# Weight copies and blocks of h formed in the projection of pair 0, in a gated pooling and attention block

## The chip, the cores and the metric

The kernel runs on 1 core of a Trainium2 chip. The metric is the device time of one execution in microseconds (us); of several executions the median is given. TensorE (PE in the profile) multiplies matrices, VectorE (DVE), ScalarE (ACT) and GpSimd (POOL) work on elements, SyncE (SP) only issues DMA transfers; ScalarE and GpSimd issue some as well. Each engine runs its own instructions in order and waits on semaphores for the others.

## What is computed

One decoder block over 1040 tokens (16 meta tokens and 1024 of the sequence) with 1024 features. All in float32:

```python
h = rmsnorm(x, norm_g)
proj = einsum('bld,dn->bln', h, w_in)
u_pool, z_pool, q, k, v, z_attn, f_logit, g_pool, g_attn = split(proj)
y_pool = causal_multiscale_pool(u_pool, pool_w, pool_scale) * silu(z_pool)
log_f = log_sigmoid(f_logit + b_forget)
y_attn = forgetting_attention(q, k, v, log_f) * silu(z_attn)   # 8 heads of 64, causal
merged = sigmoid(g_pool) * (y_pool @ w_up_pool) + sigmoid(g_attn) * (y_attn @ w_up_attn)
out = rmsnorm(x + merged @ w_out, final_norm_g)                # meta tokens dropped
```

In the attention, logit[t, s] = q_t.k_s / 8 plus the sum of log_f over s < j <= t. Before log_sigmoid, b_forget (the tile `bfb`) is added to the gate logits.

## The kernel before

Each float32 matrix product is made of three products of reduced float32 parts: hi x hi, hi x lo, lo x hi. So h is held in on-chip memory as `hh` and `hl` (the normalised tokens, high and low part, transposed), and each block of weights is loaded into `raw` and split by ScalarE (`whi`) and GpSimd (`wlo`).

The program has four stages.

1. **Front**, to about 62 us: the tokens are loaded (`xt`), normalised and transposed, and q, k and v of head pair 0 are projected in a list `todo` of twelve steps (q, k, v for four groups of tokens; `n` counts them). Then `gates()` projects the forget gates in three pieces (`pj<-hh,wfs`), copies them out (`fT`, VectorE), transposes them, adds `bfb` and forms the sums `negc`, which every logit needs. While that chain runs, TensorE is given fill work: q and k of pair 1 (`f_q`, `f_k`). The fill work writes two banks of PSUM in turn (`pj`, `PJ = 2`): q piece 1, q piece 2, then k pieces; a bank is free when ScalarE (`qa`) and VectorE (`ql`) have emptied it.
2. **16 attention units** (4 pairs x 2 heads x 2 halves of the queries), to about 430 us. The logits of a unit are made beside the softmax of the unit before, and TensorE's gaps are filled with projections: u and the gates g, whose pieces are evicted by ScalarE into staging tiles `st` (2 buffers) and stored to DRAM by SyncE (`sp_u`, `sp_gp`, `sp_ga`).
3. The remaining projections, by a Strassen-Winograd scheme of seven products (`g_prod`), to about 550 us. Its operands are sums of 512x512 blocks of h (`HS`) and of w_in (`GS`) in DRAM.
4. The up projections and the output projection, the latter by the same scheme with sums of blocks of w_out (`TD`).

The block sums for stages 3 and 4 are prepared during stage 2. `put` notes copies of weight blocks within DRAM; `move` hands them to ScalarE's queue after the exponentials (L612). `put_h` copies the high and low parts of a block of h to DRAM, where an adding transfer of GpSimd joins them; `put_neg` forms a negated block with ScalarE (L627) and GpSimd (L629). `add` is an adding transfer on GpSimd's queue (L616): it waits for a VectorE instruction (`trs`) and adds one DRAM block to another. The table `SUMS` says what happens after which unit.

The scheduler keeps TensorE's instructions in the order written; on the other queues it orders by its own estimate, except where a dependency is set with `after` or `behind`. Transfers issued by SyncE and ScalarE share eight completion semaphores: a transfer is issued only when the earlier one with its semaphore has landed.

Of the kernel before, what the change touches and what calls it, by code (L numbers as in the profile page):

```python
# [53 lines left out]
def tile_hybrid_block(ctx, tc, x, meta, norm_g, w_in, b_forget, pool_w, pool_scale,  # L54
# [92 lines left out]
    def split_w(srcs, pool=None, tags=("wh", "wl")):  # L147
        raw = wp.tile([128, KO, 128], F32, name="raw")
        k0 = 0
        for s in srcs:  # L150
            nc.sync.dma_start(raw[:, k0:k0 + s.shape[1], :], s)
            k0 += s.shape[1]
        hi = (pool or wp).tile([128, KO, 128], F32R, name="whi", tag=tags[0])
        lo = (pool or wp).tile([128, KO, 128], F32R, name="wlo", tag=tags[1])
# [7 lines left out]
    def w_chunk(col, **kw):  # L162
        return split_w([w_in2[:, :, col:col + 128]], **kw)

# [7 lines left out]

    turn, spare = [0], [True]

# [142 lines left out]
    def f_q(p):  # L317
        w = w_chunk(COL_Q + p * 128)
        alloc_q(p)
        for c0, c1 in HALVES:  # L320
            yield from q_piece(p, w, c0, c1)

    def f_k(p):
        w = w_chunk(COL_K + p * 128)
        alloc_k(p)
        for c0, c1 in PIECES:
            yield from k_piece(p, w, c0, c1)
# [10 lines left out]
    spill, stores, evacs = {}, [], []  # L338

    def f_raw(key, col):  # L340
        w = w_chunk(col)
        dt = dr.tile([128, SEQ], F32, name=f"sp_{key[0]}{key[1]}")
        spill[key] = dt
        for c0, c1 in HALVES:
            ps = yield from g_proj(w, c0, c1)
            st = stg.tile([128, 512], F32, name="st")
            evacs.append(nc.scalar.activation(st, ps, AF.Copy))
            stores.append(nc.sync.dma_start(dt[:, c0:c1], st))

    def f_u(g):  # L350
# [3 lines left out]
        for c0, c1 in PIECES:  # L354
            ps = yield from g_proj(w, c0, c1)
            st = stg.tile([128, 512], F32, name="st")[:, :c1 - c0]
# [111 lines left out]
    alloc_q(0, False)  # L468
    todo = []
# [92 lines left out]

    pw = wp.tile([128, KO, 128], F32, name="raw")[:, :4]
    nc.sync.dma_start(pw, pool_w[0].rearrange("g c d -> c g d"))
    pwh = sm.tile([128, 4, 128], F32R, name="pwh", bufs=1)
    pwl = sm.tile([128, 4, 128], F32R, name="pwl", bufs=1)

# [4 lines left out]
    for p in range(4):  # L572
        for n in ("y", "y2"):
            spill[n, p] = dr.tile([128, SEQ], F32, name=f"sp_{n}{p}")

    TD = {n: dr.tile([512, 512], F32, name=f"td{n}") for n in (1, 2, 3, 4, 5)}
    WB = {"11": w_out[0][:512, :512], "12": w_out[0][:512, 512:], "21": w_out[0][512:, :512], "22": w_out[0][512:, 512:]}

    GS = {n: dr.tile([512, 768], F32, name=f"gs{n}") for n in (1, 2, 3, 4, 5)}
    GB = {f"{r + 1}{c + 1}": (w_in[0][512 * r:512 * r + 512, z:z + 512], w_in[0][512 * r:512 * r + 512, g:g + 256])  # L580
          for r in range(2) for c, (z, g) in enumerate(((COL_ZA, COL_GA + 512), (COL_Z, COL_GA + 768)))}
    for j in range(4, 8):
        spill["ga", j] = dr.tile([128, SEQ], F32, name=f"sp_ga{j}")
    HS = {n: dr.tile([512, 512], F32, name=f"hs{n}") for n in ("11", "22", "l11", "l22", "A", "B", "C", "X")}

    accs = []

    def hblock(d, blk):
        r, c = int(blk[0]) - 1, int(blk[1]) - 1
        return r32(d[c][:, :, 512 * r:512 * r + 512])  # L590

    def rows_of(t):
        return t.rearrange("(k p) c -> p k c", p=128)

    puts, held, negs = [], [], []

    def put(dst, src):
        for r in (0, 256):
            puts.append((dst[r:r + 256], src[r:r + 256]))

    def put_g(dst, src):
        put(dst[:, :512], src[0])
        puts.append((dst[:, 512:], src[1]))

    def move(u, b):
        if b == 2 and held:
            nc.sync.dma_start(*held.pop(0))
        while b == 3 and negs:
            nc.sync.dma_start(*negs.pop(0))
        if b:  # L610
            for _ in range(-(-len(puts) // (u.nb - b))):
                after(nc.scalar.dma_start(*puts.pop(0)), exps[-1])  # L612

# [5 lines left out]

    def put_h(n):  # L620
        for d, h in ((HS[n], hh4), (HS["l" + n], hl4)):
            for k in (0, 2):
                puts.append((rows_of(d)[:, k:k + 2], hblock(h, n)[:, k:k + 2]))

    def put_neg(blk, k, *dsts):
        t = ap_.tile([128, 512], F32, name="neg", bufs=1)
        after(nc.scalar.activation(t, hblock(hh4, blk)[:, k], AF.Copy, scale=-1.0), exps[-1])  # L627
        for c in range(0, 512, 256):
            sub = nc.gpsimd.tensor_tensor(t[:, c:c + 256], t[:, c:c + 256], hblock(hl4, blk)[:, k, c:c + 256],  # L629
                                          op=ALU.subtract)  # L630
            after(sub, accs[-1])
        for d in dsts:
            negs.append((HS[d][128 * k:128 * k + 128], t))

    def n21(k):
        put_neg("21", k, "X", "A")

    def n12(k):
        put_neg("12", k, "C")

    def add_y(p):
        d, r = [spill[n, p].rearrange("(p k) c -> p (k c)", k=2) for n in ("y", "y2")]
        behind(nc.gpsimd.dma_start(d, r, accum_op=ALU.add, max_dma_last_dim=8192), trs[-1])

    SUMS = {
        0: [(put_h, "11")],
        1: [(add, HS["11"], HS["l11"]), (n21, 0), (put, TD[1], WB["11"]), (put, TD[5], WB["12"])],
        2: [(add, TD[1], TD[5]), (n21, 1), (put_h, "22")],
        3: [(add, HS["22"], HS["l22"]), (n21, 2), (put, TD[3], WB["22"])],
        4: [(add, TD[3], TD[5]), (n21, 3), (put_g, GS[1], GB["11"])],  # L650
        5: [(add, HS["X"], HS["11"]), (n12, 0), (put_g, GS[5], GB["12"])],
        6: [(add, HS["A"], HS["22"]), (n12, 1), (put_g, GS[3], GB["22"])],
        7: [(add, GS[1], GS[5]), (n12, 2), (put, HS["B"], HS["A"])],
        8: [(add, HS["B"], HS["11"]), (n12, 3), (put_g, GS[2], GB["11"])],
        9: [(add, GS[3], GS[5]), (put, TD[2], WB["11"])],
        10: [(add, HS["C"], HS["B"]), (put_g, GS[4], GB["21"])],
        11: [(add, GS[2], GS[3]), (put, TD[4], WB["21"])],
        12: [(add, TD[2], TD[3])],
        13: [(add, GS[4], GS[2])],
        14: [(add, TD[4], TD[2])],  # L660
# [14 lines left out]
    class Unit:  # L675
# [69 lines left out]
        def soft(self, b):  # L745
# [6 lines left out]
            exps.append(nc.scalar.activation(s[:kb, c0:], s[:kb, c0:], AF.Exp))  # L752
            move(self, b)
            ph = ap_.tile([128, 512], F32R, name="ph", bufs=NPH)
# [23 lines left out]
        def finish(self):  # L778
# [6 lines left out]
            else:  # L785
                nc.scalar.activation(t, po, AF.Copy)
            for n, part in (("y", hr), ("y2", lr))[:1 if self.p == 3 else 2]:
                nc.sync.dma_start(spill[n, self.p][hr, self.q0:self.q0 + 512], t[part])
            held.append((accd[:, 4 * self.p + 2 * self.e + self.half], acc))
# [30 lines left out]
    def sums_at(i, tr):  # L820
        trs.append(tr)
        sums_of(i)
        if i % 4 == 1 and i > 1:
            add_y(i // 4 - 1)

# [3 lines left out]
    for i, u in enumerate(units):  # L829
# [11 lines left out]
        u.av(u.nb - 1, 1)  # L841
        if i == 1:
            after(nc.scalar.activation(pwh, pw, AF.Copy), exps[-1])
            nc.gpsimd.tensor_tensor(pwl, pw, r32(pwh), op=ALU.subtract)
        if nxt is not None:
# [52 lines left out]
    def attn_in(p):  # L898
        y = gp.tile([128, SEQ], F32, name="y", tag="g")
        nc.sync.dma_start(y, spill["y", p])  # L900
        Y[p] = y
# [587 lines left out]
```

## Time and profile before

| | |
|---|---|
| median of 3 runs | 722.79 us (721.97 to 723.32) |
| the profiled execution | 722.44 us, its span 720.4 us |
| TensorE busy | 707.4 us (98%) |
| VectorE, ScalarE, GpSimd busy | 512.0, 425.9, 353.9 us |
| moved by DMA | 134.09 MB in packets, mean 186 GB/s |

The span runs from the first to the last instruction. In rows of the timeline the first two figures are the start and the length in us, an engine's name with a q is its queue (issuing only), and the brackets tell how long the engine was idle before and what ended it. In rows of the waits: who waited for whom, us in total, times, longest. In rows of stretches (from:to): length, busy time of PE, PEld (weight loads), DVE, ACT, POOL, then the granted TensorE clock as a share, the DMA share and GB/s. In rows of DMA issues: transfers, KB each, median us from issue to landing.

### The profile page before, as it was taken

The page shows a single profiled execution, that of the slowest core. Times are in us where ns is not written, and L with a number is a line of the kernel's source. Part 1 is how long each engine was busy: PE and PEld are TensorE (multiplying, and loading weights), DVE is VectorE, ACT ScalarE, POOL GpSimd, SP SyncE. Part 2 cuts the span into 40 slices and gives each one's busy share as a digit, 9 for nine tenths or more (in the row PEclk, how much of TensorE's full clock was granted, in tenths as well). Part 3 has the DMA queues.
Part 4 walks back from the last instruction along what each step waited for, and adds up shares of the span by engine and source line. Part 5 has one row for each costly group of instructions (what it writes and reads, how often), then busy time and mean ns, then how long its engine had stood idle before and what let it go on. Part 6 is the DMA issues. An engine that isn't in the chain of part 4 may idle for free.

```text
span 720.4 us, 10921 instructions
## 1 busy us (share of the span) xinstructions
PE 707.4 (98%) x3613; PEld 610.7 (85%) x3613; DVE 512.0 (71%) x909; ACT 425.9 (59%) x936; POOL 353.9 (49%) x481
## 2 busy tenths in 40 slices
PE   8999999799999999999999999999999999999996
PEld 6997999798889988898888888888888888888885
DVE  5743488477688767787587866899847545888775
ACT  7753577567787867777587614455646332535445
POOL 5412336477377675747388643458951010007152
PEclk9999999999999999999999999999999999999999
DMA  9211225986968889497858768799518366861006
GB/s 308 65 30 30 60 62 199 271 244 193 260 177 230 239 229 281 118 261 214 224 154 206 223 202 318 239 304 308 129 35 273 113 224 233 272 224 60 0 1 233
DMA packets 97482, 134.09 MB, mean 186 GB/s; under 512 B 11809, under 2 KB 63009, under 8 KB 95154
## 3 DMA queue, kind: packets, MB, share of 16 engines
q1 hardware_dynamic: 83296, 94.07, 40.8%
q0 software_dynamic: 2512, 18.35, 13.3%
q10 hardware_dynamic: 11618, 20.98, 8.2%
q8 instruction: 28, 0.46, 0.2%
q14 instruction: 28, 0.23, 0.1%
HBM read 103.29 MB, written 62.59 MB: 230 GB/s over the span
## 4 chain that ended last, share of the span: by engine, by line
PE 94%; ACT 2%; DMA 2%; DVE 1%; issue 1%; POOL 0%; POOLq 0%; ACTq 0%
PE pj L170 55%; PE pj L1049 12%; PE pj L1369 8%; PE po L775 5%; PE pt L1049 4%; PE pt L1369 2%; PE ps L711 2%; DMA sp_u<-st 2%; PE ps L710 2%; PE pj L521 1%; PE pt L232 1%; PE pj L711 1%; PE pj L710 1%; ACT qa L268 1%; PE pn L232 0%
## 5 line engine op out<-in xcount | busy, mean ns | idle before, releaser
L170 PE MATMUL pj<-hh,whi 128*128 128x512 f32 (+3 forms) x576 | 128.3, 350 | 0.0
L170 PE MATMUL pj<-hh,wlo 128*128 128x512 f32 (+3 forms) x576 | 127.1, 346 | 0.0
L170 PE MATMUL pj<-hl,whi 128*128 128x512 f32 (+3 forms) x576 | 126.8, 345 | 0.0
L170 PEld LDWEIGHTS pj<-hh,whi 128*128 128x128 f32 x576 | 98.4, 190 | 10.2 <-ACT hh L234 0.4
L158 POOL TENSOR_TENSOR wlo<-raw,whi 128x256 fp32r<-128x256 f32 x100 | 73.5, 774 | 65.1 <-PE pj L170 24.5
L170 PEld LDWEIGHTS pj<-hh,wlo 128*128 128x128 f32 x576 | 96.8, 188 | 10.0
L765 POOL TENSOR_TENSOR acc<-acc,S 128x256 f32<-128x256 f32 (+2 forms) x128 | 90.3, 723 | 30.5 <-ACT S L752 20.8
L170 PEld LDWEIGHTS pj<-hl,whi 128*128 128x128 f32 x576 | 96.6, 189 | 9.8
L757 DVE TENSOR_TENSOR pl<-S,ph 128x512 fp32r<-128x512 f32 (+4 forms) x112 | 80.5, 736 | 19.4 <-ACT ph L756 18.9
L1011 POOL TENSOR_TENSOR gw<-graw,gw 128x256 fp32r<-128x256 f32 x52 | 53.6, 1056 | 44.2 <-ACT gw L1004 41.8
L1049 PE MATMUL pj<-gh,gw 128*128 128x512 f32 x276 | 64.3, 389 | 0.0
L724 DVE TENSOR_TENSOR pt<-pt,S 128x400 f32<-128x400 f32 (+2 forms) x96 | 46.4, 483 | 22.1 <-ACT S L715 19.6
L1049 PEld LDWEIGHTS pj<-gh,gw 128*128 128x128 f32 x276 | 51.8, 188 | 10.9
L752 ACT ACTIVATE S<-S 128x512 f32<-128x512 f32 (+4 forms) x112 | 50.6, 479 | 8.6 <-DVE S L751 8.4
L756 ACT ACTIVATE ph<-S 128x512 fp32r<-128x512 f32 (+4 forms) x112 | 52.4, 482 | 2.3 <-PE po L775 1.4
L751 DVE TENSOR_TENSOR S<-S,pt 128x512 f32<-128x512 f32 (+4 forms) x112 | 49.7, 498 | 0.6
L1262 DVE TENSOR_TENSOR rl<-pj,rl 128x512 f32<-128x512 f32 x32 | 22.0, 689 | 28.7 <-PE pj L170 28.1
L1004 ACT ACTIVATE gw<-graw 128x512 fp32r<-128x512 f32 x38 | 23.5, 626 | 27.9 <-DMA graw<-gs 12.0
L715 ACT ACTIVATE S<-ps,negc 128x16 f32<-128x16 f32 (+4 forms) x65 | 33.0, 513 | 10.9 <-PE ps L711 10.3
L765 POOL TENSOR_TENSOR acc<-S 128x256 f32<-128x256 f32 (+1 forms) x32 | 28.6, 926 | 21.1 <-ACT S L752 17.5
L136 POOL TENSOR_TENSOR X<-G 128x256 f32<-128x256 f32 x8 | 5.8, 740 | 63.9 <-DVE G L1264 63.9
L775 PE MATMUL po<-ph,V 128*128 128x512 f32 (+4 forms) x112 | 36.6, 327 | 0.3 <-ACT ph L756 0.2
(250 smaller groups left out, 1434.2 us busy)
## 6 DMA issues: line engine op xcount, KB each, us to landing
raw<-in_w_in_dram SPq DMA_DIRECT2D x27, 512.0 KB, 5.9
gs<-in_w_in_dram ACTq DMA_DIRECT2D x15, 512.0 KB, 7.6
gs<-gs POOLq DMA_DIRECT2D x4, 1536.0 KB, 12.7
graw<-gs SPq DMA_DIRECT2D x12, 512.0 KB, 6.1
td<-in_w_out_dram ACTq DMA_DIRECT2D x10, 512.0 KB, 11.4
graw<-in_w_in_dram SPq DMA_DIRECT2D x9, 512.0 KB, 6.9
xt<-in_x_dram SPq DMA_DIRECT2D x8, 512.0 KB, 6.3
accd<-acc SPq DMA_DIRECT2D x16, 256.0 KB, 4.2
```

Source lines behind the costliest of these rows:

```text
L158: ins = nc.gpsimd.tensor_tensor(lo[:, k:k + 2], raw[:, k:k + 2], r32(hi[:, k:k + 2]), op=ALU.subtract)
L170: nc.tensor.matmul(ps, a, b, start=(i == 0), stop=(i == len(seq) - 1))
L724: nc.vector.tensor_tensor(m[:kb, c0:], m[:kb, c0:], s[:kb, c0:], op=ALU.max)
L751: nc.vector.tensor_tensor(s[:kb, c0:], s[:kb, c0:], self.pm[:kb, c0:], op=ALU.subtract)
L752: exps.append(nc.scalar.activation(s[:kb, c0:], s[:kb, c0:], AF.Exp))
L756: nc.scalar.activation(ph[:kb, c0:], s[:kb, c0:], AF.Copy)
L757: dves.append(nc.vector.tensor_tensor(pl[:kb, c0:], s[:kb, c0:], r32(ph[:kb, c0:]), op=ALU.subtract))
L765: accs.append(nc.gpsimd.tensor_tensor(acc[:kb, c:c1], (S0 if b == 1 else acc)[:kb, c:c1], s[:kb, c:c1], op=ALU.add))
L775: nc.tensor.matmul(self.po[:, c0:], v, self.P[b][i][:kb, c0:], start=(b == 0 and i == 0), stop=(b == self.nb - 1 and i == 1))
L1011: nc.gpsimd.tensor_tensor(op[:, 1, k:k + 2], raw[:, k:k + 2], r32(op[:, 0, k:k + 2]), op=ALU.subtract)
L1049: nc.tensor.matmul(ps, stat(n, i, p, k), op_h[n][q][k // 2][:, k % 2], start=fresh and m == 0, stop=m == 11, skip_group_check=True)
L1369: nc.tensor.matmul(ps, pick(A_, k, p)[:, i * 128:(i + 1) * 128], pick(B_, k, q)[:, c0:c1], start=start and n == 0, stop=n == 11, skip_grou ...
```

## The change

- The tables `TD`, `GS`, `HS` and the copies are set up before the front. The copies of weight blocks are issued by SyncE: seven after each of the steps n = 4, 5 and 6 (21 copies of 512 KB), and the last four, one each behind a later weight load (`w_chunk`). None is issued by ScalarE in the units.
- The weights of q and k of pair 1 are loaded after n = 5 and 6 (`early`).
- After n = 8 to 11 VectorE forms one block of h each (`h_block`): hi + lo, or -hi - lo, in two instructions over 128x1024 elements into tiles `f`, which SyncE stores to `HS` (ten stores of 512 KB, since block 21 goes to two places). The copies of the parts, the two adds that joined them and the negations in the units are gone. The tiles `f` take the buffers of `xt` (tag `s`, 6), which later hold the logits S.
- pool_w is loaded after n = 7 into such a buffer and no longer into `raw`; its high part is formed after n = 10 and no longer in unit 1.
- A third of the staged pieces goes to a third buffer (the one that `neg` had).
- The halves y and y2 of a head lie in one DRAM tile, so a unit stores them in one DMA; `SUMS` has one adding transfer in each unit.

Cut to its core:

```diff
+    HS = {n: dr.tile([512, 512], F32, name=f"hs{n}") for n in ("11", "22", "A", "B", "C", "X")}
+    def h_block(blk):
+        neg = blk in ("12", "21")
+        for k in (0, 2):
+            f = ap_.tile([128, 2, 512], F32, name="f", tag="s", bufs=6)
+            hi, lo = [hblock(d, blk)[:, k:k + 2] for d in (hh4, hl4)]
+            if neg:
+                nc.vector.scalar_tensor_tensor(f, hi, -1.0, lo, op0=ALU.mult, op1=ALU.subtract)
+            else:
+                nc.vector.tensor_tensor(f, hi, lo, op=ALU.add)
+            dsts = [HS[{"11": "11", "22": "22", "12": "C", "21": "X"}[blk]]] + ([HS["A"]] if blk == "21" else [])
+            for d in dsts:
+                nc.sync.dma_start(rows_of(d)[:, k:k + 2], f)
+    def copies(n, prev=None):
+        for _ in range(min(n, len(puts))):
+            ins = nc.sync.dma_start(*puts.pop(0))
+            if prev is not None:
+                after(ins, prev)
+    put_g(GS[5], GB["12"])
+    put_g(GS[1], GB["11"])
...
+    def w_chunk(col, raw=None):
+        if raw is None:
+            raw = wp.tile([128, KO, 128], F32, name="raw")
+            copies(1, nc.sync.dma_start(raw, w_in2[:, :, col:col + 128]))
...
+    def piece():
+        turn[1] += 1
+        if turn[1] % 3:
+            return stg.tile([128, 512], F32, name="st")
+        return ap_.tile([128, 512], F32, name="st3", tag="neg", bufs=1)
...
+        if n == 5:
+            early["q"] = load_raw(COL_Q + 128)
+        if n == 6:
+            early["k"] = load_raw(COL_K + 128)
+        if 3 < n < 7:
+            copies(7)
+        if n == 7:
+            pw = ap_.tile([128, 4, 128], F32, name="pw", tag="s", bufs=6)
+            nc.sync.dma_start(pw, pool_w[0].rearrange("g c d -> c g d"))
+        if n == 10:
+            nc.scalar.activation(pwh, pw, AF.Copy)
+            nc.gpsimd.tensor_tensor(pwl, pw, r32(pwh), op=ALU.subtract)
+        if n > 7:
+            h_block(("11", "12", "22", "21")[n - 8])
...
-        if b:
-            for _ in range(-(-len(puts) // (u.nb - b))):
-                after(nc.scalar.dma_start(*puts.pop(0)), exps[-1])
...
-        0: [(put_h, "11")],
-        1: [(add, HS["11"], HS["l11"]), (n21, 0), (put, TD[1], WB["11"]), (put, TD[5], WB["12"])],
-        2: [(add, TD[1], TD[5]), (n21, 1), (put_h, "22")],
...
+        0: [(add, GS[1], GS[5])],
+        1: [(add, GS[3], GS[5])],
+        2: [(add, TD[1], TD[5])],
...
```

**SyncE's queue in the front.** In the program before, the rows behind the token loads (`bfb` and `psc` are the forget biases and the pool scale, then weights, then the first stores of u):

```order
L497 DMA wf<-in_w_in_dram 128x8x8
L508 DMA bfb<-in_b_forget_dram 128x8
L509 DMA psc<-in_pool_scale_dram 128x4x1
L564 DMA raw<-in_pool_w_dram 128x4x128
L151 DMA raw<-in_w_in_dram 128x8x128 x4
L359 DMA sp_u_988<-st 128x384 x2
```

In the changed program 21 copies and two weight loads follow wf, and then:

```order
L567 DMA pw<-in_pool_w_dram 128x4x128
L181 DMA hs_137<-f 128x2x512 x2
L205 DMA raw<-in_w_in_dram 128x8x128
L185 DMA td_128<-in_w_out_dram 256x512
L181 DMA hsC<-f 128x2x512 x2
L205 DMA raw<-in_w_in_dram 128x8x128
L181 DMA hs_138<-f 128x2x512 x2
L181 DMA hsX<-f 128x2x512
L181 DMA hsA<-f 128x2x512
L181 DMA hsX<-f 128x2x512
L181 DMA hsA<-f 128x2x512
L579 DMA bfb<-in_b_forget_dram 128x8
```

bfb has moved from the second place behind the token loads to the place behind all stores of h.

**VectorE at the end of the front.** Before, from the split of the gate weights (`wfs`) to the copies of the gate pieces (`fT`):

```order
L501 TENSOR_TENSOR wfs<-wf,wfs 128x8x8
L272 SCALAR_TENSOR_TENSOR ql<-pj,qa 64x256 x2
L290 TENSOR_TENSOR ka<-pj,ka 64x256
L290 TENSOR_TENSOR ka<-pj,ka 64x16
L290 TENSOR_TENSOR ka<-pj,ka 64x256
L290 TENSOR_TENSOR ka<-pj,ka 64x16
L315 TENSOR_TENSOR V<-pj,V 128x2x64 x2
L524 COPY fT<-pj 16x384 x2
```

Now:

```order
L558 TENSOR_TENSOR wfs<-wf,wfs 128x8x8
L178 TENSOR_TENSOR f<-hh_123,hl_124 128x1024 x2
L322 SCALAR_TENSOR_TENSOR ql<-pj,qa 64x256 x2
L176 SCALAR_TENSOR_TENSOR f<-hh_125,hl_126 128x1024 x2
L340 TENSOR_TENSOR ka<-pj,ka 64x256
L340 TENSOR_TENSOR ka<-pj,ka 64x16
L340 TENSOR_TENSOR ka<-pj,ka 64x256
L340 TENSOR_TENSOR ka<-pj,ka 64x16
L178 TENSOR_TENSOR f<-hh_125,hl_126 128x1024 x2
L365 TENSOR_TENSOR V<-pj,V 128x2x64 x2
L176 SCALAR_TENSOR_TENSOR f<-hh_123,hl_124 128x1024 x2
L595 COPY fT<-pj 16x384 x2
```

Eight instructions that form h blocks stand between those of the projection. The sixth waits for the store of the first (its buffer), the seventh for that of the second, and the last for GpSimd's use of pw.

**ScalarE in unit 1.** Before, from a staged piece of u (`st`) on, with softmax (S, ph) and the copies of blocks of w_out:

```order
L357 ACTIVATE st<-pj 128x272
L752 ACTIVATE S<-S 128x272
L612 DMA td_781<-in_w_out_dram 256x512
L756 ACTIVATE ph<-S 128x272
L752 ACTIVATE S<-S 128x144
L612 DMA td_785<-in_w_out_dram 256x512
L715 ACTIVATE S<-pj,negc 128x512
L752 ACTIVATE S<-S 128x16
```

Now, from the same piece on:

```order
L413 ACTIVATE st_1736<-pj 128x272
L774 ACTIVATE S<-S 128x144
L774 ACTIVATE S<-S 128x16
L209 ACTIVATE whi<-raw 128x512 x2
L737 ACTIVATE S<-pj,negc 128x512
L744 ACTIVATE pt<-S 128x512
L737 ACTIVATE S<-ps,negc 128x512 x2
```

The copies are gone from ScalarE, and the piece goes to the third staging buffer. TensorE's order is the same in both programs.

More of the change, by code (lines that the diff above doesn't have):

```diff
@@ new lines, in hblock, with rows_of, put, put_g @@
+    def hblock(d, blk):
+        r, c = int(blk[0]) - 1, int(blk[1]) - 1
+        return r32(d[c][:, :, 512 * r:512 * r + 512])
+    def rows_of(t):
+        return t.rearrange("(k p) c -> p k c", p=128)
+    puts, held, negs = [], [], []
+    def put(dst, src):
+        for r in (0, 256):
+            puts.append((dst[r:r + 256], src[r:r + 256]))
+    def put_g(dst, src):
+        put(dst[:, :512], src[0])
+        puts.append((dst[:, 512:], src[1]))
+    def h_block(blk):
[10 more added lines that the diff above has]
+                nc.sync.dma_start(rows_of(d)[:, k:k + 2], f)
@@ L468, in tile_hybrid_block @@
     alloc_q(0, False)
-    todo = []
+    pwh, pwl = [sm.tile([128, 4, 128], F32R, name=n, bufs=1) for n in ("pwh", "pwl")]
+    todo, early = [], {}
     for t0, t1 in ((0, 256), (256, 512), (512, 768), (768, L)):
@@ L561, in gates @@
         F.pull(LATENCY)
[L563 to L566, printed above, removed]
     exps, dves = [], []
@@ L572, in tile_hybrid_block, with add, move @@
     for p in range(4):
[L573 to L581, printed above, removed]
+        spill["y", p] = dr.tile([128 if p == 3 else 256, SEQ], F32, name=f"sp_y{p}")
     for j in range(4, 8):
         spill["ga", j] = dr.tile([128, SEQ], F32, name=f"sp_ga{j}")
-    HS = {n: dr.tile([512, 512], F32, name=f"hs{n}") for n in ("11", "22", "l11", "l22", "A", "B", "C", "X")}
     accs = []
[L588 to L605, printed above, removed]
+    def add(dst, src):
+        d, r = [t.rearrange("r c -> (r c)").rearrange("(p m) -> p m", m=2048) for t in (dst, src)]
+        behind(nc.gpsimd.dma_start(d, r, accum_op=ALU.add, max_dma_last_dim=8192), trs[-1])
+    trs = []
+    def move(b):
         if b == 2 and held:
@@ L625, in put_neg @@
[L625 to L633, printed above, removed]
@@ L899, in attn_in @@
         y = gp.tile([128, SEQ], F32, name="y", tag="g")
-        nc.sync.dma_start(y, spill["y", p])
+        if p == 3:
+            nc.sync.dma_start(y, spill["y", p])
+        else:
+            for e in range(2):
+                nc.sync.dma_start(y[rows(e)[0]], spill["y", p].rearrange("(n r) c -> n r c", n=4)[2 * e])
         Y[p] = y
```

87 lines of the change are left out of this document (40 added, 47 removed).

## The prediction

> **What bounds the kernel now.** I read the page first, then TensorE's waits, then the stretch in which it waits, engine by engine, and last the front of the program, where the change puts its work.
>
> ```profile
> PE 707.4 (98%) x3613; PEld 610.7 (85%) x3613; DVE 512.0 (71%) x909; ACT 425.9 (59%) x936; POOL 353.9 (49%) x481
> DMA  9211225986968889497858768799518366861006
> ```
>
> TensorE is busy for 707.4 of 720.4 us, so no edit on another engine gains anything unless TensorE waits for it. The DMA row shows the opposite picture: after the second slice (18 us each) the engines are nearly idle up to 108 us, and later mostly full.
>
> ```profile
> PE pj L710 <- ACT S L715: 4.1, 1, 4.1
> ...
> 136.00:138.00 2.00, 0.42 (x3) 0.10 (x1) 0.00 (x0) 0.00 (x0) 0.00 (x0) 1.00 0.90 314
> 138.00:140.00 2.00, 0.00 (x0) 0.00 (x0) 0.00 (x0) 0.20 (x1) 0.00 (x0) 1.00 1.06 389
> 140.00:141.00 1.00, 0.47 (x2) 0.42 (x3) 0.00 (x0) 1.00 (x3) 0.22 (x1) 1.00 1.14 346
> 141.00:144.00 3.00, 3.00 (x11) 2.83 (x10) 2.01 (x3) 2.81 (x6) 0.12 (x1) 0.51 1.06 291
> 144.00:145.00 1.00, 1.00 (x5) 0.90 (x5) 0.09 (x1) 0.47 (x1) 1.00 (x2) 0.76 1.00 383
> ```
>
> TensorE has one wait of weight, 4.1 us at 136 to 140.5 us. The granted clock (third figure from the end) then stands at 0.51 for 3 us and 0.76 for 1 us, which costs 3 x 0.49 + 0.24 = 1.7 us more. So 5.8 us is all that can be won in the units. Who held it:
>
> ```profile
> 126.66 1.06 POOL L616 DMA_DIRECT2D hs<-hsl  x1
> 128.03 11.14 DMA sp_u<-st
> 139.19 0.50 ACTq L612 DMA_DIRECT2D td<-in_w_out_dram  x1
> 139.79 0.69 ACT L715 ACTIVATE S<-pj,negc 128x512 f32<-128x512 f32 x1 [7.55 <-DMA sp_u<-st]
> ...
> sp_u<-st SPq DMA_DIRECT2D x8, 192.0 KB, 2.7
> hs<-hsl POOLq DMA_DIRECT2D x2, 1024.0 KB, 11.3
> gs<-gs POOLq DMA_DIRECT2D x4, 1536.0 KB, 12.7
> ```
>
> ScalarE stops at 132.2 (139.79 - 7.55) in front of a weight copy that it issues itself at 139.19. The copy waits until the store issued at 128.03 has landed (128.03 + 11.14 = 139.17): the two share a completion semaphore. That store usually lands in 2.7 us; here GpSimd's adding transfer, issued at 126.66, filled the DMA engines. ScalarE's evictions (L715) queue behind the copy, and TensorE behind them.
>
> **The change, part by part.**
>
> Out of the units go 25 weight copies and 8 copies of h on ScalarE's queue, 8 negations on ScalarE and 16 subtractions on GpSimd.
>
> ```profile
> L612 ACTq DMA_DIRECT2D gs<-in_w_in_dram x15: 497/497/503, 198.9 to 324.0; - x15
> L627 ACT ACTIVATE neg<-hh x8: 614/628/636, 123.9 to 265.6; 128x512 f32<-128x512 f32 x8
> L629 POOL TENSOR_TENSOR neg<-neg,hl x16: 722/738/749, 125.3 to 267.0; 128x256 f32<-128x256 f32 x16
> ```
>
> That is about 15 us of issuing (33 x 0.37 to 0.50), 5.0 us of ScalarE and 11.8 us of GpSimd. All of it lay beside TensorE's fill work but for the one wait, so I price it at that wait: **minus 5.8 us**. ScalarE issues no copy in the units now, so nothing there can hang on a store's landing in this way. Next in line is staging: the first adds now move 1.5 MB (12.7 us) in units 0 and 1, when a projected piece is stored every 4 to 5 us. Three buffers cover 13 us, two would not; price nothing, and the cover is the third buffer. The adding transfers go from 17 to 15, at most one a unit, and the y halves are stored in one DMA instead of two; nothing waits for them: zero. pwh moves from unit 1 to the front (0.6 us of ScalarE, 1.3 of GpSimd); it waits for pw, at about 53 us by the sums below, and the work behind it, V and vt, is not needed before 60.9: zero.
>
> Into the front come, all on SyncE's queue: 21 copies and the weights of q and k of pair 1, then pw, then ten stores of h blocks with two more weight loads and one copy between them, and only then bfb, the forget biases, which was an early load:
>
> ```profile
> 16.38 0.43 SPq L497 DMA_DIRECT2D wf<-in_w_in_dram  x1
> 16.86 0.58 SPq L508 DMA_DIRECT2D bfb<-in_b_forget_dram  x1
> ...
> 2.00:18.00 16.00, 15.45 (x75) 11.19 (x74) 9.59 (x16) 12.60 (x24) 8.26 (x12) 1.00 1.07 344
> 24.00:50.00 26.00, 26.00 (x223) 25.78 (x223) 16.31 (x35) 16.29 (x41) 7.65 (x14) 1.00 0.01 2
> 244.00:247.00 3.00, 3.00 (x15) 2.51 (x14) 1.64 (x4) 2.02 (x5) 2.08 (x3) 1.00 1.06 402
> ```
>
> From 24 to 50 us the engines move 2 GB/s; the room is there. But one queue's transfers go one after another, so bfb lands after everything ahead of it: 36 transfers of 0.524 MB and pw's 0.26 make 19.1 MB. The rate is bounded by two rows, 344 GB/s (the loads at the start) and 402 (mostly such copies, at 244 to 247 us). I take 375, near the copies' row because 32 of 36 are copies and stores with long rows. The first copy follows wf, from about 19.5 us. Then bfb lands at 19.5 + 19.1/0.375 + 1 = 71.4 us (68.0 at 402 and 76.0 at 344; a landing is put at 1 us).
>
> The Trainium skill ("DMA: Bandwidth & Descriptors", section "Where 436 GB/s comes from") gives about 358 GB/s as one core's limit to its memory; by it the estimate for bfb would be 73.9 us, and the whole sum 2.5 us worse. This case's 402 GB/s in copies within the same memory does not show that limit.
>
> Who waits for bfb, in the trace of before:
>
> ```profile
> 52.29 0.49 DVE L315 TENSOR_TENSOR V<-pj,V 128x128 fp32r<-128x128 f32 x2
> 56.34 0.55 DVE L524 COPY fT<-pj 16x384 f32<-16x384 f32 x1 [3.55 <-PE pj L521]
> 64.29 0.23 DVE L535 TENSOR_TENSOR fz<-pt,bfb 128x72 f32<-128x72 f32 x1 [1.29 <-PE pt L529]
> 67.74 0.59 DVE L545 RECIPROCAL fz<-fz 128x72 f32<-128x72 f32 x1
> 70.37 1.39 DVE L272 SCALAR_TENSOR_TENSOR ql<-pj,qa 64x512 fp32r<-64x512 f32 x2 [0.96 <-ACT qa L268]
> ...
> 58.92 1.16 PE L521 MATMUL pj<-hh,wfs 128*16 128x272 f32 x8
> 73.16 1.57 PE L170 MATMUL pj<-hh,whi 128*128 128x384 f32 x8
> ...
> 67.92 2.41 ACT L268 ACTIVATE qa<-pj 64x512 fp32r<-64x512 f32 x4 [0.99 <-PE pj L170]
> ...
> L912 DVE TENSOR_TENSOR y<-y,rc 128x1024 f32<-128x1024 f32 x4 | 5.4, 1350 | 0.0
> L938 DVE SCALAR_TENSOR_TENSOR u<-s,u 128x1024 f32<-128x1024 f32 x4 | 6.4, 1596 | 0.1
> ```
>
> VectorE adds bfb at 64.29 and is ready for ql 4.0 us later (67.74 + 0.59); one qa of 0.6 us now stands in ScalarE's part of that chain: 4.6. The two ql, 1.4 us, with a small step between them, empty the bank: about 6.3 us after bfb. TensorE needs that bank (of two) at 73.16 for the first piece of k of pair 1. With bfb at 71.4 it gets it at 77.7, **4.5 us late**; with 68.0, 1.1 us; with 76.0, 9.1 us. TensorE's order is unchanged, so nothing else is slid in.
>
> VectorE's own work comes before that. Eight instructions over 1024 columns, four at 1.35 and four at 1.6 us, are 11.8 us between 44 and 61 us, where it mostly idles. In my walk through its queue two delay ka's low half by 1.7 us; one waits for the first h store to land (about 55) and stands ahead of V's low half; two more (3.2 us) stand between V and the first fT copy, which ends near 61 instead of 56.9. TensorE's third gate piece needs that bank at 58.92: **2 us late**. This is not added: the wait for bfb ends at a set time, so the later of the two counts. Between them TensorE stands still for some 2.5 us in front of the k piece. The only drop of the clock here followed 4.1 us of waiting, so I add none; bounds 0 and 1.7.
>
> The Trainium skill ("TensorE: Matmul & The Clock Gate", section "Part 1: The HAM clock gate (the "warmup" mystery)") has the clock halved after an idle window of about 3.4 us, in windows that run free. The trace agrees: 4.1 us idle, then 0.51. By that rule a wait of 2.5 us loses nothing and one of 7 us must lose about 1.7.
>
> **Sum** against the profiled execution (722.4 us, 720.4 of span and 2.0 around it): 722.4 - 5.8 + 4.5 = 721.1. The median of the runs, 722.8, is 0.4 above that execution: **721.5 us** forecast. 0.2% (1.4 us) is about what a measurement of this kernel can tell from no change: 721.35 to 724.25 is the same.
>
> **The rivals.**
>
> - *The front hides it.* If bfb is in by 69 us, only VectorE's 2 us are left: 722.8 - 5.8 + 2.0 = 719.0. For it: 402 GB/s gives 68.0, and the eight instructions may fit VectorE's gaps better than my walk. Against: three ordinary loads are among the transfers, and the start shows 344 with such loads.
> - *The front costs more than the units gain.* At 344 GB/s bfb lands at 76.0; TensorE stands 7 us, and the clock drops: 722.8 - 5.8 + 9.1 + 1.7 = 727.8. It is slower once bfb comes after about 72.5 with a clock drop, 74.1 without. For it: the row of the start, and each queue slot freed only when an earlier transfer has landed; against: the copies' 402.
> - *The wait at 136 us stays*, held by staging or by the weight behind a longer add: 722.8 + 4.5 = 727.3. For it: 12.7 us against 11.3. Against: what stopped ScalarE was its own copy, and that is gone.
>
> **How the numbers follow.** The likeliest, bfb at 70 to 73.5 with no or little clock loss, gets 0.50 and its own range is 720.1 to 723.7; 0.17 of it lies below 721.35. The hidden front gets 0.26. The costly front gets 0.19, of which 0.02 within 0.2%. The wait that stays gets 0.05. Faster 0.17 + 0.26 = 0.43; same 0.33 + 0.02 = 0.35; slower 0.17 + 0.05 = 0.22. The range, 718.7 to 726.5, cuts the far ends of the outer two.
>
> **What would show it.** Right: no wait on ScalarE near 136 us and no clock at 0.51 there; DMA slices 2 to 4 full; VectorE's first fz instruction waiting for bfb at about 71 us; TensorE's longest wait in front of the first k piece, for VectorE's ql, at 2 to 5 us. Wrong: bfb before 69 or after 74, a clock drop after that wait, or a new wait in units 0 to 2 for staging or weights.

## The result, and the profile after

The changed kernel takes **740.82 us** in the median (739.47 to 741.22, 4 runs), the program before 723.0 us (721.97 to 723.32, 4 runs): ratio 1.0246, 95% interval 1.0228 to 1.0263. It is slower by 17.8 us, where 721.5 was forecast and 726.5 was the top of the range.

From the page of the changed kernel: the span, the engines' busy time, and the rows of 40 slices (18.4 us each) for TensorE, its clock and the DMA engines.

```profile
span 737.8 us, 10901 instructions
...
PE 712.2 (97%) x3613; PEld 614.1 (83%) x3613; DVE 519.7 (70%) x917; ACT 421.0 (57%) x928; POOL 344.1 (47%) x463
...
PE   9996699999999999999999999998999999999996
...
PEclk9998899999999999999999999999999999999999
DMA  9998523674644657443757557989706457671006
```

DMA slices 2 to 4 are full, as the change intends. But TensorE has holes in slices 4 and 5 and in slice 28, and its clock drops in 4 and 5. Its waits, by what ended them:

```profile
PE pj L592 <- DVE V L365: 6.3, 1, 6.3
PE pj L220 <- DVE ql L322: 6.2, 1, 6.2
PE pj L1072 <- DVE gx L1083: 4.1, 1, 4.1
PE pn L475 <- DVE car L628: 1.3, 1, 1.3
```

The wait for ScalarE's S at 136 us is gone. Three stand in its place: at 56.6 to 62.9 us before the second gate piece, at 81.8 to 88.0 us before the first piece of u, and at 496.2 to 500.2 us in stage 3. The prediction and the description of the front take the piece of the second wait for one of k of pair 1. It is of u: in the program before, ScalarE evicts the piece that starts at 73.16 us into a staging buffer. The bank and the time are the same, so no sum hangs on the name.

```profile
77.55 0.49 ACT L357 ACTIVATE st<-pj 128x384 f32<-128x384 f32 x1 [1.78 <-PE pj L170]
```

Stretches of the changed kernel's trace around the three waits (the granted clock is the third figure from the end):

```profile
60.00:66.00 6.00, 3.06 (x10) 1.42 (x11) 4.94 (x6) 1.82 (x6) 3.02 (x3) 0.50 0.90 322
...
88.00:93.00 5.00, 4.99 (x16) 5.00 (x17) 2.35 (x5) 0.46 (x1) 0.42 (x1) 0.50 0.67 206
...
500.00:503.00 3.00, 2.77 (x7) 2.25 (x8) 3.00 (x5) 1.63 (x3) 1.09 (x1) 0.51 1.06 337
```

After each wait TensorE runs at half clock.

**Who held the first two waits.** VectorE's rows (the bracket tells how long it was idle and what ended that):

```profile
60.54 1.73 DVE L178 TENSOR_TENSOR f<-hh,hl 128x1024 f32<-128x1024 f32 x1 [5.78 <-DMA hs<-f]
62.30 0.49 DVE L365 TENSOR_TENSOR V<-pj,V 128x128 fp32r<-128x128 f32 x2
...
81.25 0.23 DVE L606 TENSOR_TENSOR fz<-pt,bfb 128x72 f32<-128x72 f32 x1 [9.80 <-DMA bfb<-in_b_forget_dram]
...
497.46 0.58 DVE L997 TENSOR_REDUCE fin<-fin 128x64 f32<-128x256 f32 x1 [4.35 <-DMA fin<-sums]
```

The sixth h block waits 5.78 us until the first store of h has landed (its buffer), and V's low half stands behind it. The second gate piece needs the bank that V's low half empties: that is the first wait. VectorE then waits 9.80 us for bfb; ql follows some 6 us later, and the bank comes free at 87.9: the second. Third, VectorE waits for the load of the softmax sums (fin). Why bfb is late stands in SyncE's queue and in the rates of two stretches:

```profile
58.52 1.26 SPq L181 DMA_DIRECT2D hsC<-f  x2
67.75 0.37 SPq L205 DMA_DIRECT2D raw<-in_w_in_dram  x1
...
74.04 1.24 SPq L579 DMA_DIRECT2D bfb<-in_b_forget_dram  x1
```

```profile
20.00:45.00 25.00, 25.00 (x216) 24.76 (x215) 19.33 (x39) 16.94 (x41) 7.36 (x15) 1.00 1.03 328
...
65.00:68.00 3.00, 3.00 (x17) 1.57 (x15) 0.94 (x3) 0.00 (x0) 2.94 (x5) 0.74 0.19 72
```

The copies, with the loads among them, move at 328 GB/s, not 375. From 59.8 to 67.75 SyncE issues nothing: it stands before a weight load whose buffer `raw` GpSimd still reads (its split, `wlo`, ends at 67.72). So the engines run dry (72 GB/s at 65 to 68 us), and bfb, behind all h stores, is issued at 74.04 and lands at 81.16.

**Where the time went.** As TensorE's lost time I count, for each matmul, the time from its start to the next start, less the median of its shape; half clock is in it. Worked out from one trace of each kernel, so the medians beside it need not follow it to the last 2 us:

| kernel | median us | lost, 40 to 100 us | 120 to 160 | 460 to 520 | all |
|---|---|---|---|---|---|
| before | 723.0 | 0.7 | 6.5 | -0.1 | 17.5 |
| changed | 740.82 | 18.0 | 0.6 | 5.8 | 34.6 |
| bfb first | 731.33 | 7.7 | 0.6 | 4.1 | 22.4 |
| nine copies in the front | 726.54 | 2.7 | 2.5 | 5.3 | 21.1 |
| last piece elsewhere | 736.62 | 19.3 | 0.7 | 1.6 | 31.5 |
| two staging buffers | 735.70 | 16.4 | 1.5 | 1.5 | 29.4 |
| copies from two queues | 741.61 | 20.4 | 0.8 | 5.4 | 36.6 |
| pool_w first | 739.75 | 19.9 | 0.8 | 1.5 | 32.9 |
| before, copies by SyncE | 726.79 | 0.7 | 7.7 | -0.1 | 21.8 |
| before, no first add | 720.63 | 0.7 | 5.7 | -0.1 | 16.4 |
| fifteen copies | 719.31 | 1.9 | 2.1 | 0.7 | 14.8 |
| fifteen, rest early | 718.07 | 1.9 | 0.6 | 1.8 | 14.4 |
| the same, two staging buffers | 720.58 | 1.5 | 1.9 | 1.4 | 15.7 |

Of the changed kernel: -5.9 at 136 us, +17.3 in the front, +5.9 at 496 us, together +17.3; the spans differ by 17.4.

### The profile page after: what moved, and what is told of

It reads as the page before. It is cut to its first block, busy times and chain, and to the rows that moved or that the text cites. A ratio compares the mean times of both kernels' runs of the same rounds, so it can differ in the third digit from the quotient of the medians.

```text
span 737.8 us, 10901 instructions
## 1 busy us (share of the span) xinstructions
PE 712.2 (97%) x3613; PEld 614.1 (83%) x3613; DVE 519.7 (70%) x917; ACT 421.0 (57%) x928; POOL 344.1 (47%) x463
## 4 chain that ended last, share of the span: by engine, by line
PE 81%; DMA 6%; DVE 5%; ACT 3%; issue 2%; SPq 1%; POOL 0%; POOLq 0%; DVEq 0%; ACTq 0%
PE pj L220 50%; PE pj L1392 8%; PE pj L1072 7%; PE po L797 5%; PE pt L1392 2%; PE pt L1072 2%; PE ps L733 2%; PE ps L732 2%; DMA hs<-f 1%; DMA sums<-ge 1%; DMA bfb<-in_b_forget_dram 1%; DVE pl L779 1%; ACT qa L318 1%; PE pj L592 1%; PE pt L282 1%
## 5 line engine op out<-in xcount | busy, mean ns | idle before, releaser
L220 PE MATMUL pj<-hh,wlo 128*128 128x512 f32 (+3 forms) x576 | 127.5, 347 | 0.0
L211 POOL TENSOR_TENSOR wlo<-raw,whi 128x256 fp32r<-128x256 f32 x100 | 75.0, 780 | 74.4 <-ACT whi L209 53.4
L779 DVE TENSOR_TENSOR pl<-S,ph 128x512 fp32r<-128x512 f32 (+4 forms) x112 | 80.2, 737 | 15.5 <-ACT ph L778 14.8
L1034 POOL TENSOR_TENSOR gw<-graw,gw 128x256 fp32r<-128x256 f32 x52 | 50.8, 1005 | 50.3 <-ACT gw L1027 49.2
L1072 PE MATMUL pj<-gh,gw 128*128 128x512 f32 x276 | 65.9, 396 | 4.1 <-DVE gx L1083 4.1
L1072 PEld LDWEIGHTS pj<-gh,gw 128*128 128x128 f32 x276 | 52.9, 192 | 15.7 <-issue 4.4
L746 DVE TENSOR_TENSOR pt<-pt,S 128x400 f32<-128x400 f32 (+2 forms) x96 | 46.5, 485 | 19.9 <-ACT S L737 17.6
L1392 PE MATMUL pj<-opw 128*128 128x512 f32 (+1 forms) x168 | 36.2, 374 | 0.0
```

Source lines behind the costliest of these rows:

```text
L220: nc.tensor.matmul(ps, a, b, start=(i == 0), stop=(i == len(seq) - 1))
L746: nc.vector.tensor_tensor(m[:kb, c0:], m[:kb, c0:], s[:kb, c0:], op=ALU.max)
L779: dves.append(nc.vector.tensor_tensor(pl[:kb, c0:], s[:kb, c0:], r32(ph[:kb, c0:]), op=ALU.subtract))
L1034: nc.gpsimd.tensor_tensor(op[:, 1, k:k + 2], raw[:, k:k + 2], r32(op[:, 0, k:k + 2]), op=ALU.subtract)
L1072: nc.tensor.matmul(ps, stat(n, i, p, k), op_h[n][q][k // 2][:, k % 2], start=fresh and m == 0, stop=m == 11, skip_group_check=True)
L1392: nc.tensor.matmul(ps, pick(A_, k, p)[:, i * 128:(i + 1) * 128], pick(B_, k, q)[:, c0:c1], start=start and n == 0, stop=n == 11, skip_grou ...
```

## The experiments

**1. bfb and psc first.**

```diff
             nc.sync.dma_start(wf, w_in2[:, :, COL_F:COL_F + H])
+            nc.sync.dma_start(bfb, bass.AP(tensor=b_forget.tensor, offset=b_forget.offset, ap=[[0, 128], [1, H]]))
+            nc.sync.dma_start(psc, pool_scale[0].rearrange("(g c) -> c g", c=128))
```

> The changed kernel (740.8 us) with one edit: bfb and psc are loaded right behind wf, ahead of the copies. Theory: the second wait of the front (6.2 us at 81.4 to 88.0 us) and the half clock after it (2.9 us) hang on bfb alone, which landed at 81.2; VectorE would reach the instruction that needs it at 71.5, and ql 6.3 us later, before TensorE needs the bank: 740.8 - 9.1 = 731.7 us. The first wait (V, 6.3 us) stays. Rival: VectorE and the weights behind the eight h blocks are as late anyway, then ql comes as late as before and the time stays at 740.8.

Measured 731.33 us (730.62 to 732.13), 9.5 below the changed kernel. Its waits of TensorE, then VectorE's first rows that need bfb and free the bank:

```profile
PE pj L592 <- DVE V L365: 8.2, 1, 8.2
PE pj L1072 <- DVE gx L1083: 2.2, 1, 2.2
```

```profile
75.15 0.23 DVE L606 TENSOR_TENSOR fz<-pt,bfb 128x72 f32<-128x72 f32 x1 [1.29 <-PE pt L600]
...
81.22 1.39 DVE L322 SCALAR_TENSOR_TENSOR ql<-pj,qa 64x512 fp32r<-64x512 f32 x2 [0.96 <-ACT qa L318]
```

The wait for ql is gone: VectorE waits 1.29 us for TensorE instead of 9.80 for bfb. So bfb's place in the queue is shown to be the second wait. The first stays, and is longer here (8.2 us).

**2. Nine copies in the front.**

```diff
+    put(TD[3], WB["22"])
     put_g(GS[2], GB["11"])
-    put(TD[3], WB["22"])
...
-            copies(7)
+            copies(3)
...
-            copies(1, nc.sync.dma_start(raw, w_in2[:, :, col:col + 128]))
+            copies(2, nc.sync.dma_start(raw, w_in2[:, :, col:col + 128]))
```

> The changed kernel with 9 copies in the front (three after each of n = 4, 5, 6) instead of 21; the others follow later weight loads, two behind each, and TD[3] goes ahead of GS[2]. The h blocks on VectorE stay as they are. Theory: both waits of the front come from the copies ahead in the one queue; 12 copies fewer at 331 GB/s are 19 us, so bfb lands near 62 us and the first h store as soon as it is formed: no wait for V or ql, 740.8 - 18.0 (the three stretches from 40 to 100 us) = 722.8 us; only the wait at 495 us is left. Rival A: VectorE's eight instructions by themselves hold V or fT; then a wait of 2 us (my prediction's figure) to 6 us stays before 64 us: 724.8 to 731.6. Rival B: the copies behind the loads hold weights or staged stores in units 0 to 2, a new wait there.

Measured 726.54 us (724.37 to 727.4). The waits of TensorE, and VectorE's wait for bfb:

```profile
PE pj L1072 <- DVE gx L1083: 3.7, 1, 3.7
PE pj L732 <- ACT S L737: 1.5, 1, 1.5
...
PE pj L220 <- DVE ql L322: 1.1, 1, 1.1
...
PE pj L592 <- DVE fT L595: 0.2, 1, 0.2
```

```profile
69.83 0.23 DVE L606 TENSOR_TENSOR fz<-pt,bfb 128x72 f32<-128x72 f32 x1 [5.28 <-DMA bfb<-in_b_forget_dram]
```

The wait for V is gone with all eight h blocks still on VectorE, so rival A falls: the blocks by themselves cost 0.2 us of waiting (L592), and the copies ahead of their stores were the first wait. Still 3.7 us more than I expected: bfb came at 69.8 and not 62 (the loads' own copies go ahead of it), and the copies left over met the adding transfer of unit 1, 2.5 us at 120 to 160 us. That is rival B.

**3. The last staged pieces.**

```diff
-        if turn[1] % 3:
+        if turn[1] % 3 or turn[1] > 33:
             return stg.tile([128, 512], F32, name="st")
```

> The changed kernel with one edit: the last three staged pieces of the units do not use the third staging buffer (36 pieces, and the 36th is one of its turns). Theory: that buffer lies in memory that the tiles zp take over in stage 3, so the loads of the softmax sums wait for the store of the last piece, the chain of eight sums starts 5 us late and ends at the wait of 4.1 us at 495 us with 1.7 us of half clock behind it: 740.8 - 5.8 = 735.0 us, and SyncE issues the two loads ahead of the last two stores. Rival: the sums are late from slower transfers (the y loads are two now instead of one), then the wait stays and so do 740.8 us.

Measured 736.62 us (735.57 to 736.92), 4.2 less. SyncE's rows there, of the changed kernel and then of this one:

```profile
436.49 6.02 SPq L404 DMA_DIRECT2D sp_ga<-st  x3
446.46 0.80 SPq L978 DMA_DIRECT2D zp<-accd  x2
```

```profile
438.49 1.35 SPq L978 DMA_DIRECT2D zp<-accd  x2
439.90 5.58 SPq L404 DMA_DIRECT2D sp_ga<-st  x2
```

The loads of the sums (zp) no longer wait for the store of the last piece, and of 5.8 us lost in stage 3 4.2 are gone. That the third buffer holds these loads is shown by the order. Its price is less sure: with the buffer in use and the loads again behind the last store, the wait in stage 3 is 2.2 us in the trace of run 1 and 1.4 us in that of run 8, no longer than the 1.4 us here. What holds the remaining 1.6 us is not tried.

**4. In the program before: the copies issued by SyncE.**

```diff
-                after(nc.scalar.dma_start(*puts.pop(0)), exps[-1])
+                after(nc.sync.dma_start(*puts.pop(0)), exps[-1])
```

> The program before with one edit: the copies in the units are issued by SyncE instead of ScalarE, at the same places behind the same exponentials. Theory: the wait at 136 us was ScalarE's own copy hanging on a store's landing; without it 722.8 - 5.8 = 717.0 us, with no granted clock of 0.51 there. Rival: the adding transfer of GpSimd itself holds the staged store, then ScalarE waits for the staging buffer (or a weight load behind the copies) nearly as long: 721 to 723, or slower than 722.8 where SyncE, held in front of a copy, issues stores and loads late.

Measured 726.79 us (726.12 to 726.98): slower than before, ratio 1.005 (1.0035 to 1.0065). TensorE's wait, and ScalarE's row at its end:

```profile
PE pj L710 <- ACT S L715: 5.2, 1, 5.2
PE ps L710 <- ACT S L715: 1.6, 1, 1.6
```

```profile
139.45 0.40 ACT L357 ACTIVATE st<-pj 128x272 f32<-128x272 f32 x1 [6.53 <-DMA sp_u<-st]
```

```profile
126.85 2.31 SPq L151 DMA_DIRECT2D raw<-in_w_in_dram  x2
129.27 1.00 SPq L359 DMA_DIRECT2D sp_u<-st  x2
```

The rival's second half came true. ScalarE issues no copy and stops all the same, now before an eviction whose buffer is not stored. SyncE's order has changed with the copies: the store of the piece of 122.6 us, issued at 122.79 in the program before, now stands behind the stores of neg and two weight loads. It is issued at 129.27, just behind the adding transfer (128.70), and lands 10.1 us later. So this run shows what copies do to SyncE's queue; whether ScalarE's own copy was the hang it leaves open, since two buffers are held here where it was one.

**5. In the program before: without the first add.** The sum of the two parts of block 11 is left out.

```diff
-        1: [(add, HS["11"], HS["l11"]), (n21, 0), (put, TD[1], WB["11"]), (put, TD[5], WB["12"])],
+        1: [(n21, 0), (put, TD[1], WB["11"]), (put, TD[5], WB["12"])],
```

> The program before without the adding transfer of unit 1 (the sum of the two parts of h's block 11 is left out, so that block is its high part alone). Theory after the run with SyncE's copies: the adding transfer is the root; it holds the staged store of 128.0 us, and ScalarE's copy or the staging buffer are only the two places where that store is waited for. Without it the wait of 5.8 us goes: 722.8 - 5.8 = 717.0 us, the store lands in 2 to 6 us. Rival: the two copies that ScalarE issues at 129.3 and 130.9 and the stores around them hold the store as well; then a wait of 3 us or more stays and the time is 720 to 723.

Measured 720.63 us (718.64 to 721.61), ratio 0.9959 (0.9944 to 0.9973): 2.5 us less, not 5.8.

```profile
PE pj L710 <- ACT S L715: 3.4, 1, 3.4
```

```profile
140.00:144.00 4.00, 4.00 (x15) 3.76 (x14) 2.14 (x4) 3.49 (x8) 1.10 (x2) 0.57 1.02 258
```

```profile
138.81 0.69 ACT L715 ACTIVATE S<-pj,negc 128x512 f32<-128x512 f32 x1 [6.80 <-DMA raw<-in_w_in_dram]
```

A wait of 3.4 us and its half clock stay, as the rival had it. The store of 129.78 still takes 9.6 us, among two weight copies, a weight load and two stores of y. ScalarE's copy (138.21 now) again stands ahead of S after 6.8 us of idling, but here it waits for another transfer: the weight load issued at 129.31, which lands at 138.19. So the adding transfer is not the root: without it, copies and loads hold one another nearly as long.

**6. The changed kernel with two staging buffers.**

```diff
-        if turn[1] % 3:
-            return stg.tile([128, 512], F32, name="st")
-        return ap_.tile([128, 512], F32, name="st3", tag="neg", bufs=1)
+        return stg.tile([128, 512], F32, name="st")
```

> The changed kernel with the two staging buffers of before for all pieces. Theory: with two buffers a staged store held by an adding transfer (12.7 us) stops ScalarE in front of the next eviction, as it does in the program before; the third buffer is what took away the wait at 136 us, not the copies that left ScalarE. Then one wait of 4 to 6 us with its half clock comes back in units 0 to 3, and the wait at 495 us loses the 4.2 us measured: 740.8 + 5.8 - 4.2 = 742.4 us. Rival: taking the copies off ScalarE was the cure; then no wait in the units and 740.8 - 4.2 = 736.6.

Measured 735.70 us (734.75 to 737.17): the rival.

```profile
PE pj L590 <- DVE V L365: 7.4, 1, 7.4
PE pj L220 <- DVE ql L322: 5.8, 1, 5.8
...
PE pj L1070 <- DVE gx L1081: 1.3, 1, 1.3
PE pj L730 <- ACT S L735: 0.3, 1, 0.3
```

```profile
152.80 0.68 ACT L735 ACTIVATE S<-pj,negc 128x512 f32<-128x512 f32 x1
154.05 1.25 ACT L735 ACTIVATE S<-ps,negc 128x512 f32<-128x512 f32 x2
157.22 0.49 ACT L411 ACTIVATE st<-pj 128x384 f32<-128x384 f32 x1 [1.92 <-DMA sp_u<-st]
```

These are the same pieces of unit 1 as at 127.5 to 142.8 us in the program before. The adding transfer (144.60, 12.4 us) holds the first piece's store about as long as there: 146.94 to 157.14, 10.2 us. But ScalarE's evictions of S pass at 152.8 to 155.3 us, ahead of the one that needs the buffer, and that one waits 1.9 us; TensorE waits 0.3 us in all the units. With the same late store and the same two buffers, what is missing is the copy in ScalarE's queue ahead of S. That bears the prediction's reading out, and the cover it named was not needed.

**7. Copies from two queues.**

```diff
-            ins = nc.sync.dma_start(*puts.pop(0))
+            turn[2] += prev is None
+            ins = (nc.gpsimd if turn[2] % 2 else nc.sync).dma_start(*puts.pop(0))
```

> The changed kernel with every second copy of the front issued by GpSimd instead of SyncE. Theory of one queue: one queue alone does not get more than 331 GB/s out of the engines; with two the rate over 20 to 45 us is 380 or more, bfb lands near 70 us instead of 81.2 and both waits of the front shrink: 728 to 733 us. Rival: the memory or the engines are the limit; the rate stays at 320 to 340 GB/s, SyncE's transfers get half of it while GpSimd's run, bfb lands at 76 to 81 and the time stays within 3 us of 740.8.

Measured 741.61 us (740.87 to 742.22).

```profile
20.00:45.00 25.00, 25.00 (x216) 24.76 (x215) 19.35 (x38) 16.71 (x41) 12.68 (x25) 1.00 1.05 338
```

Two queues get 338 GB/s where one got 328, with the DMA engines' share at 1.05 and 1.03. So a second issuing queue does not lift the rate; what bounds it is not shown. The rival had bfb at 76 to 81 us, and that was off: VectorE waits for it until 83.50, so TensorE's second wait grows to 11.0 us, while the first shrinks to 3.7.

**8. pool_w first.** Its load moves from behind n = 7 to behind wf.

```diff
             nc.sync.dma_start(wf, w_in2[:, :, COL_F:COL_F + H])
+            pw = ap_.tile([128, 4, 128], F32, name="pw", tag="s", bufs=6)
+            nc.sync.dma_start(pw, pool_w[0].rearrange("g c d -> c g d"))
...
-        if n == 7:
-            pw = ap_.tile([128, 4, 128], F32, name="pw", tag="s", bufs=6)
-            nc.sync.dma_start(pw, pool_w[0].rearrange("g c d -> c g d"))
```

> The changed kernel with pool_w loaded right behind wf, ahead of the copies, and nothing else moved (bfb stays late). Theory: the first wait of the front is held by the sixth h block, which waits until the first store of h has landed behind the copies (60.5 us); pool_w only held ScalarE beside it. Then ScalarE's wait of 8 us for pwh goes and TensorE's stays at 6 us: 740.8 us within 1. Rival: ScalarE, held in front of pwh, is the holder (it forms V's high part behind it); then the first wait goes: 740.8 - 8.8 = 732.0.

Measured 739.75 us (737.84 to 741.56): in the main the theory. ScalarE forms pwh at 51.9 us, and VectorE's sixth block still waits for the first h store; TensorE's wait stays, 8.3 us here:

```profile
63.62 1.23 DVE L178 TENSOR_TENSOR f<-hh,hl 128x1024 f32<-128x1024 f32 x1 [8.21 <-DMA hs<-f]
```

```profile
PE pj L591 <- DVE V L365: 8.3, 1, 8.3
...
PE pj L1071 <- DVE gx L1082: 1.4, 1, 1.4
```

The last line was not expected: the wait in stage 3 is 1.4 us instead of 4.1, though nothing there was changed and the zp loads are still issued behind the last stores (447.00 us). The trace is of the fastest of four executions (737.84 us), so the others may have more of it.

**9. Fifteen copies.** Runs 1 and 3 together, and `copies(5)` for `copies(7)`.

> The changed kernel with three edits: bfb and psc loaded right behind wf, the last three staged pieces kept out of the third buffer, and 15 copies in the front (five after each of n = 4, 5, 6), the other 10 one behind each later weight load. Theory: 6 copies fewer ahead bring pw from 59.2 to 49.7 us and the first h store from 60.5 to 51 (6 x 1.58 us), so neither ScalarE's pwh nor VectorE's sixth h block waits and the first wait of the front goes (8.8 us with its half clock); the second goes with bfb (9.2, measured 9.5), the third shrinks as measured (4.2): 740.8 - 22.2 = 718.6 us, 4.2 below the program before. Rival A: the copies left over meet an adding transfer in unit 1 as in the kernel with nine copies, a wait of 1.6 us: 720.2. Rival B: the h blocks themselves are the first wait; then 740.8 - 13.4 = 727.4.

Measured 719.31 us (717.86 to 719.65), ratio to the program before 0.994 (0.9927 to 0.9953). That lies between the theory (718.6) and rival A (720.2). Behind the start no wait above 1.0 us is left:

```profile
PE pj L732 <- ACT S L737: 1.0, 1, 1.0
PE pj L592 <- DVE fT L595: 0.6, 1, 0.6
PE pj L1072 <- DVE gx L1083: 0.5, 1, 0.5
```

**10. The rest early.** As run 9, and `copies(3, ...)` behind each later weight load for `copies(1, ...)`.

> The kernel with fifteen copies in the front (719.3 us), and the other 10 copies three behind each later weight load instead of one, so that all are issued before about 92 us, ahead of the first adding transfer (106.6 us). Theory: the wait left in its unit 1 (1.0 us and 0.8 of small steps at 141 to 145 us) comes from a copy, an adding transfer and the stores in one stretch of the DMA engines; without copies there it goes: 717.5 us. Rival: the adding transfer of 1.5 MB alone holds the third staged store; then the wait stays and so do 719.3 us. Second rival: three copies in a row hold the weights of u: a new wait of 1 to 3 us at 75 to 100 us, 719 to 721.

Measured 718.07 us (717.25 to 718.98), ratio 0.9934 (0.9918 to 0.9949). The loss at 120 to 160 us falls from 2.1 to 0.6 us, as expected, but a wait of 1.6 us stands in stage 3, so the whole is not measurably better than run 9. It beats both kernels.

**11. Run 10 with two staging buffers** (the edit of run 6, without that of run 3).

> The kernel of the run before in this call (15 copies in the front, the rest early, bfb first), with the two staging buffers of before for all pieces. Theory, from the run of the changed kernel with two buffers: the third buffer is worth under 1 us where no copies run in the units: the same within 1 us (717.5 to 718.5). Rival: the shorter front lets staging meet the adding transfers at a worse place and a wait of 2 to 6 us comes back in units 0 to 3: 720 to 724.

Measured 720.58 us (718.44 to 721.44), ratio 0.9962 (0.9947 to 0.9978), 2.5 us above run 10 on the same chip. That is the rival's time, but not its wait: TensorE's losses add up to only 1.3 us more, 1.3 of them at 120 to 160 us. The ratios' intervals overlap by a hair, so the third buffer's worth, once the front is mended, is not settled better than 1 to 2.5 us.

## Why the prediction was wrong, step by step

The steps that failed are the landing of bfb (71.4 us forecast, 81.16 measured), the clock behind the second wait, and stage 3, where no step had looked. Added to the forecast they give 721.5 + 6.8 + 3.0 + 0.5 + 2.9 + 5.9 = 740.6 us, where 740.82 was measured; the 0.5 is the piece's start at 88.0 instead of 87.5.

- **"Minus 5.8 us" at 136 us: right in size**, 5.9 by the table. The reason, ScalarE's own copy behind a late store, fits run 6, where the store is as late (10.2 us) and TensorE hardly waits without that copy. Why the store was late was told too narrowly: without the adding transfer copies and loads hold it 9.6 us, and ScalarE's copy hung on a weight load instead (run 5). Run 4, meant to take the copy away alone, changed SyncE's order as well.
- **"I take 375, near the copies' row": mis-sized, +6.8 us.** At 331 GB/s over 20 to 50 us, 19.1 MB end at 19.5 + 57.7 + 1 = 78.2 us, not 71.4; the lower bound of 344 was already too high. The 402 came from a row of 3 us. In it packets of 2 KB took 84 ns each (16 engines: 390 GB/s), in the front 99 ns in the mean of 20 to 50 us (330), where a tenth of them took over 110 ns. The Trainium skill ("DMA: Bandwidth & Descriptors", "Where 436 GB/s comes from") has 358; I set it aside for the 402. It was nearer, and still above what this front gave.
- **One queue "goes one after another": a step left out, +3.0 us.** I counted bytes ahead of bfb and named only the freeing of queue slots as a risk. A weight load among them waited for GpSimd to free `raw`, and everything behind it waited too. That this is the whole rest (81.2 against 78.2) is read from the trace; only moving bfb past it was tried (run 1).
- **"About 6.3 us after bfb": right.** 81.2 + 6.3 = 87.5, and the piece starts at 88.0 where it started at 73.2. "The later of the two counts" held as well: both waits and the half clock between them end in those 14.9 us.
- **The first wait: seen and mis-sized.** The prediction had the sixth block wait for a store landing at 55; it landed at 60.45, from the same slow copies, and 2 us became 6.3. They were not lost where it said, at the third gate piece behind the fT copy, but at the second, behind V's low half. pw, put at 53, landed at 59.2 and stopped ScalarE for 8.0 us; run 8 shows that this held nothing by itself. The first wait alone would not have set the end, as the step said; but with bfb early it does (run 1).
- **"I add none" for the clock: wrong, +2.9 us** behind the second wait. Waits of 3.4 to 4.1 us were followed by 3.4 us at half clock, those of 5.2 to 8.3 us by 6.8 (once, in run 1, by 10.2); the bound of 1.7 was one such stretch. The Trainium skill ("TensorE: Matmul & The Clock Gate", "Part 1: The HAM clock gate (the "warmup" mystery)") has the clock halved after an idle window of about 3.4 us, in windows that run free, and the prediction took from it that a wait of 2.5 us loses nothing. The traces differ: behind a wait of only 2.2 us in run 1 (489.5 to 491.7 us) the granted clock was 0.50 from 493.0 to 496.4. Waits of 1.0 to 1.6 us lost nothing more (runs 8, 9 and 10).
- **"Price nothing, and the cover is the third buffer": wrong twice.** It was not needed as cover in the changed kernel (run 6), and it held the loads of stage 3, where no step had looked: its pool's memory is taken over by zp. The median falls by 4.2 us without that (run 3) and by 5.1 without the buffer (run 6); the wait itself differs between traces, 1.4 to 4.1 us with the buffer in use.
- Of the rivals, the costly front came true, at the place named, with a price of 17.3 us instead of 10.8; the 5.9 us of stage 3 stood in none.

## What to carry to other kernels

Idle DMA engines are room in the engines and not in a queue: price a move by what stands behind it in the same queue, put small loads that a chain needs ahead of bulk, and ask of every instruction in the queue what it may wait for. Take a transfer rate from a stretch as long as the one you forecast, with the same packets. A buffer added in one stage can tie two stages together through the memory that the next stage reuses; look who gets it.

## What was not expected of the hardware

- The transfers of the front, mostly copies within DRAM in packets of 1 and 2 KB, ran at 328 to 338 GB/s over 25 us, from one queue or from two; 402 was measured over 3 us only. In those 3 us nearly every packet of 2 KB took 84 ns. In the front the median is 84 ns as well, but a tenth took over 110 and the longest 1704 ns. Why is not shown.
- A store of 192 KB, 2.7 us in the median, takes about 10 us beside an adding transfer of 1.5 MB without any copy (run 6) and beside two copies, a load and stores without an adding transfer (run 5). What that costs depends on what waits for it: 0.3 us of TensorE in run 6, 4.1 and half clock before.
- A wait of 6.2 us cost twice: 6.2 us and then 6.8 us at half clock, of which 2.9 were lost. A wait of 2.2 us was enough for 3.4 us at half clock (run 1).
